# Both state products of a chunk pair at one step in a state-space scan

## The chip, the cores and the metric

The kernel runs on one core of a Trainium2 chip. Its engines are TensorE (PE, with its weight loads as PEld), VectorE (DVE), ScalarE (ACT), GpSimd (POOL) and SyncE (SP, which issues all DMA transfers of this kernel). Each engine works through its own queue in order and waits on semaphores for what another engine or a transfer has to deliver. The metric is the time of one execution on the device in microseconds: the median of the runs.

## The reference, cut to what matters

Two layers follow each other over 2048 tokens of width 1024, all in float32: a Mamba-2 layer and a sliding-window attention layer. The change is in the Mamba-2 layer's scan. There are 8 groups of 4 heads, and per group the sequence is cut into 16 chunks of 128 tokens:

```
states = einsum('bclgn,bcgrl,bclgrp->bcgrpn', Bc, decay_to_end, x)   # one per chunk
chunk_decay = exp(a_cs[..., -1])
def step(h, inp):
    s, d = inp
    return h * d[..., None, None] + s, h                              # h: state BEFORE the chunk
_, h_in = scan(step, h0, (states, chunk_decay))
y_off = einsum('bclgn,bcgrpn,bcgrl->bclgrp', Cc, h_in, exp(a_cs))
y_diag = einsum('bcgrls,bcsgrp->bclgrp', cb * decay, x)
```

A chunk's output reads the state before it (`h_in`), so the state after the very last chunk is computed by the recurrence but read by nothing.

## The kernel before, in words

The sequence is worked in two halves (`hf` 0 and 1) of 1024 tokens, and each half in 8 head groups (`g`). For a group, `ssm_proj` makes six projections B, C, x0, x1, z0, z1, each over two blocks of 512 tokens. A float32 product is made from a high and a low part of each factor in three matmuls (`mm3`, lines 90 to 92: high by high, high by low, low by high). The weights come by DMA (`wraw`), ACT rounds the high part (`whi`, line 150) and POOL subtracts for the low part (`wlo`, line 152). The results are `ps` in PSUM; ACT and DVE turn them into `sx` (convolution and SiLU, lines 736 to 750) or `zz`.

While the projections of one group run, the scan of the group before it runs beside them: `interleave` takes one of the 14 steps of the generator `ssm_scan` after so much projection work. The eight chunks c of a half are handled in pairs. `stage1(c)` transposes x and B of a chunk into PSUM (`pt`, lines 776 to 778) and makes C by B (line 779); DVE forms `xd` and `xw` (lines 783, 786); ACT and POOL split `xw` into `xh` and `xl` (lines 789, 791), ACT and DVE split B into `bh` and `bl` (lines 793, 795). ACT also makes the decays `dec` from `ab`, a row of cumulated decays that a DMA spreads over all partitions (line 764), and `ce`, which takes the place of `ab` (lines 800 to 808).

`state(c)` then makes the chunk's state product `sps` with `mm3`, of 256 columns, in the PSUM tag "st" of one buffer, multiplies the state before it with the chunk's decay on POOL (`hd`, line 820) and adds the two on DVE (`hn`, line 821; line 816 copies where there is no state yet). `outputs(c)` makes the outputs of a pair in `yt` (lines 833 and 838): it reads `dec` and `xd`, and the state before each chunk with `ce`, so for a pair (c, c+1) it needs hn of c-1 and of c. Only after it are the buffers of `ab` free for the loads of chunks c+4 and c+5. The steps of a group are: stage1(0), stage1(1), then for each pair state(c) with stage1(c+2), state(c+1) with stage1(c+3), and outputs(c).

The order of the instructions on each engine is made when the program is built, by a scheduler that takes them by priority as written and by its own estimates. The scan of the last group has no projections beside it but the first pieces of the output projection (`out_piece`), whose weights `out_load` splits on ACT and DVE (lines 222 and 223).

Of the kernel before, what the change touches and what calls it, by code (L numbers as in the profile page):

```python
# [21 lines left out]
P = 128  # L22
# [38 lines left out]
class Trunk:  # L61
# [691 lines left out]
    def ssm_scan(self, sp, yp, tabs, hf, g, res, yT):  # L753


        nc = self.nc
        dt, acs, cd, w2, atd = (tabs[k] for k in ("dt", "acs", "cd", "w2", "atd"))
        abs_, sts = [], []

        def load(c):  # L760
            if c < 8:
                ab = sp.tile([P, 4, P], F32, tag="ab", name="ab", bufs=4)
                j = c * 8 + g
                nc.sync.dma_start(ab.rearrange("p r l -> p (r l)"), atd[j].partition_broadcast(P))
                abs_.append(ab)

        def stage1(c):
            if c > 7:
                return
            ab = abs_[c]  # L770
            s, o = divmod(c, 4)
            sl = slice(o * P, (o + 1) * P)
            x0, x1, Bt, Ct = (res[n, s] for n in ("x0", "x1", "B", "C"))
            pt = (yp.tile([P, 4, P], F32, tag="y", name="pt", bufs=2) if c % 2
                  else self.tp.tile([P, 4, P], F32, tag="tr", name="pt"))
            nc.tensor.transpose(pt[:, 0, :], x0[:, sl], self.ident)
            nc.tensor.transpose(pt[:, 1, :], x1[:, sl], self.ident)
            nc.tensor.transpose(pt[:, 2, :], Bt[:, sl], self.ident)
            nc.tensor.matmul(pt[:, 3, :], Bt[:, sl], Ct[:, sl], start=True, stop=True)
            xv = pt[:, 0:2, :].rearrange("p a (h d) -> p (a h) d", d=64)  # L780
            xd = sp.tile([P, 4, 64], F32, tag="xd", name="xd", bufs=4)
            hb = dt[:, c, 4 * g:4 * g + 4].unsqueeze(2).to_broadcast([P, 4, 64])
            nc.vector.tensor_tensor(xd, xv, hb, ALU.mult)
            xw = sp.tile([P, 4, 64], F32, tag="xw", name="xw", bufs=1)
            hb = w2[:, c, 4 * g:4 * g + 4].unsqueeze(2).to_broadcast([P, 4, 64])
            nc.vector.tensor_tensor(xw, xv, hb, ALU.mult)
            xf = xw.rearrange("p h d -> p (h d)")
            xh = sp.tile([P, 256], F32R, tag="xh", name="xh")
            nc.scalar.activation(xh, xf, AF.Copy)
            xl = sp.tile([P, 256], F32R, tag="xl", name="xl")  # L790
            nc.gpsimd.tensor_tensor(xl, xf, xh.bitcast(F32), ALU.subtract)
            bh = sp.tile([P, P], F32R, tag="bh", name="bh")
            nc.scalar.activation(bh, pt[:, 2, :], AF.Copy)
            bl = sp.tile([P, P], F32R, tag="bl", name="bl")
            nc.vector.tensor_tensor(bl, pt[:, 2, :], bh.bitcast(F32), ALU.subtract)
            cbm = sp.tile([P, P], F32, tag="cbm", name="cbm", bufs=1)
            nc.vector.tensor_tensor(cbm, pt[:, 3, :], self.triu, ALU.mult)
            dec = sp.tile([P, 4, P], F32, tag="dec", name="dec", bufs=4)
            for r in range(4):
                nc.scalar.activation(dec[:, r, :], ab[:, r, :], AF.Relu, scale=-1.0,  # L800
                                     bias=acs[:, c, 4 * g + r:4 * g + r + 1])
            ce = None
            if not (hf == 0 and c == 0):
                ce = ab
                nc.scalar.activation(ce, ab, AF.Exp)  # L805
                nc.gpsimd.tensor_tensor(ce, ce, Ct[:, sl].unsqueeze(1).to_broadcast([P, 4, P]), ALU.mult)  # L806
            nc.scalar.activation(dec, dec, AF.Exp, scale=-1.0)
            nc.vector.tensor_tensor(dec, dec, cbm.unsqueeze(1).to_broadcast([P, 4, P]), ALU.mult)
            sts.append((xd, (bh, bl, xh, xl), dec, ce))

        def state(c, hprev):
            sps = yp.tile([P, 256], F32, tag="st", name="sps")
            self.mm3(sps, *sts[c][1], True, True)
            hn = self.hsave[g] if (hf == 0 and c == 7) else sp.tile([P, 256], F32, tag="hst", name="hn", bufs=3)
            if hprev is None:
                nc.vector.tensor_copy(hn, sps)
            elif not (hf == 1 and c == 7):
                hb = cd[:, c, 4 * g:4 * g + 4].unsqueeze(2).to_broadcast([P, 4, 64])
                hd = sp.tile([P, 4, 64], F32, tag="hd", name="hd", bufs=1)
                nc.gpsimd.tensor_tensor(hd, hprev.rearrange("p (h d) -> p h d", d=64), hb, ALU.mult)  # L820
                nc.vector.tensor_tensor(hn, hd.rearrange("p h d -> p (h d)"), sps, ALU.add)
            return hn

        def outputs(c0, hps):

            yt = yp.tile([P, 2, 2 * P], F32, tag="y", name="yt", bufs=2)
            for u in range(2):
                xd, _, dec, ce = sts[c0 + u]
                for pr in range(2):
                    yo = yt[:, pr, u * P:(u + 1) * P]  # L830
                    for e in range(2):
                        r = 2 * pr + e
                        nc.tensor.matmul(yo[64 * e:64 * e + 64], xd[:, r, :], dec[:, r, :],  # L833
                                         start=True, stop=ce is None)
                    if ce is not None:
                        for e in range(2):
                            r = 2 * pr + e
                            nc.tensor.matmul(yo[64 * e:64 * e + 64], hps[u][:, 64 * r:64 * r + 64], ce[:, r, :],  # L838
                                             start=False, stop=True)
            s, o = divmod(c0, 4)  # L840
            sl = slice(o * P, (o + 2) * P)
            ysb = sp.tile([P, 2, 2 * P], F32, tag="ysb", name="ysb")
            for pr in range(2):
                yv = ysb[:, pr, :]
                nc.vector.scalar_tensor_tensor(yv, res[f"x{pr}", s][:, sl], self.dch[:, 2 * g + pr:2 * g + pr + 1],  # L845
                                               yt[:, pr, :], ALU.mult, ALU.add)
                nc.gpsimd.tensor_tensor(yv, yv, res[f"z{pr}", s][:, sl], ALU.mult)  # L847
            t0 = (8 * hf + c0) * P
            nc.sync.dma_start(
                yT[2 * g * P:(2 * g + 2) * P, t0:t0 + 2 * P].rearrange("(a p) t -> p a t", p=P), ysb)  # L850

        for c in range(4):
            load(c)
        stage1(0)
        yield
        stage1(1)
        yield
        hprev = self.hsave[g] if hf else None
# [174 lines left out]
```

## Time and profile before

| what | value |
| --- | --- |
| median of 3 runs | 2682.56 us (2681.83 to 2687.38) |
| profiled execution | 2682.86 us, of it the span 2681.2 us |
| PE busy | 2570.6 us, 96% |
| PEld busy | 2142.0 us, 80% |
| DVE busy | 1707.9 us, 64% |
| ACT busy | 1266.6 us, 47% |
| POOL busy | 1051.0 us, 39% |
| mean granted TensorE clock | 0.982 |

The span is the time from the first to the last instruction of the profiled execution; the rest of its time lies around it. Busy time is the time in which an engine has an instruction under way. [...] Matmuls are pipelined: a product of 512 columns has a record of 0.39 us, but the next one starts 0.23 us after it, so starts are compared and not records. The scans of the Mamba-2 layer lie between about 100 and 1495 us.

### The profile page before, as it was taken

Reading aid. Unit: us, or ns where it says so; the run is one execution under the profiler, and the core shown is the slowest. Engines: PE = TensorE matmul, PEld = TensorE weight load, DVE = VectorE, ACT = ScalarE, POOL = GpSimd, SP = SyncE. Lnnn points to the kernel's source line nnn. Section 1 sums busy time; section 2 is a strip of 40 time slices with the busy share of each in tenths; the row PEclk is TensorE's granted clock in tenths of the full one; section 3 lists DMA queues with packets and bytes.
Section 4 is the critical chain, followed back from the end, with each engine's and each line's share of the span. In section 5 each row is a group of like instructions: output and inputs, shape, how many; then the busy total and the mean of one; then the engine's idle time right before and its main releaser. Section 6 shows DMA issues by size and latency. Waiting matters only on the chain.

```text
span 2681.2 us, 39280 instructions
## 1 busy us (share of the span) xinstructions
PE 2570.6 (96%) x14307; PEld 2142.0 (80%) x14307; DVE 1707.9 (64%) x3484; ACT 1266.6 (47%) x3015; POOL 1051.0 (39%) x885
## 2 busy tenths in 40 slices
PE   7999999999999899999999999999999999999998
PEld 6877877778777777877787788888888888888787
DVE  6668665766786566666668644447766776767522
ACT  4555455555554455545556432334554454554321
POOL 2354454545544555555556322223222122221222
PEclk9999999999999999999999999999999999999999
DMA  4322222222313222222224432235111131101343
GB/s 122 94 86 67 77 71 78 68 71 75 112 52 108 68 68 74 75 73 71 66 77 137 141 99 97 95 100 170 52 52 40 52 91 52 56 27 52 111 150 121
DMA packets 266658, 224.49 MB, mean 84 GB/s; under 512 B 31136, under 2 KB 229984, under 8 KB 266464
## 3 DMA queue, kind: packets, MB, share of 16 engines
q1 hardware_dynamic: 266464, 221.98, 27.6%
q8 instruction: 113, 1.85, 0.3%
q14 instruction: 81, 0.66, 0.1%
HBM read 179.72 MB, written 42.21 MB: 83 GB/s over the span
## 4 chain that ended last, share of the span: by engine, by line
PE 71%; DVE 10%; DMA 5%; ACT 5%; issue 4%; POOL 4%; SPq 0%; ACTq 0%; POOLq 0%; DVEq 0%
PE u L251 18%; PE ps L90 13%; PE ps L91 13%; PE ps L92 13%; DMA ab<-atd 4%; DVE sx L746 4%; PE sc L421 2%; POOL wlo L152 2%; PE yt L833 2%; PE yt L838 1%; PE ot L467 1%; ACT dec L800 1%; PE tt L449 1%; PE tq L388 1%; PE ot L471 1%
## 5 line engine op out<-in xcount | busy, mean ns | idle before, releaser
L90 PE MATMUL ps<-hi,whi 128*128 128x512 f32 (+1 forms) x1808 | 732.2, 405 | 1.0 <-ACT hi L139 1.0
L92 PE MATMUL ps<-hi,wlo 128*128 128x512 f32 (+1 forms) x1808 | 710.1, 393 | 2.9 <-POOL wlo L152 2.9
L91 PE MATMUL ps<-lo,whi 128*128 128x512 f32 (+1 forms) x1808 | 709.4, 392 | 0.3 <-DVE lo L140 0.3
L92 PEld LDWEIGHTS ps<-hi,wlo 128*128 128x128 f32 x1808 | 344.2, 190 | 79.8 <-POOL wlo L152 4.3
L90 PEld LDWEIGHTS ps<-hi,whi 128*128 128x128 f32 x1808 | 346.0, 191 | 71.5 <-issue 9.4
L91 PEld LDWEIGHTS ps<-lo,whi 128*128 128x128 f32 x1808 | 346.0, 191 | 60.7 <-DVE lo L140 0.8
L746 DVE SCALAR_TENSOR_TENSOR sx<-raw,cw,sx 128x512 f32<-128x512 f32 x384 | 378.0, 985 | 20.2 <-ACT sx L743 17.5
L152 POOL TENSOR_TENSOR wlo<-wraw,whi 128x1024 fp32r<-128x1024 f32 x114 | 282.5, 2478 | 160.2 <-ACT whi L150 151.4
L800 ACT ACTIVATE dec<-ab,acs 128x128 f32<-128x128 f32 x512 | 168.1, 392 | 170.8 <-DMA ab<-atd 160.5
L251 PE MATMUL u<-oh,yh 128*128 128x512 f32 x768 | 241.7, 395 | 0.0
L251 PE MATMUL u<-ol,yh 128*128 128x512 f32 x768 | 239.1, 392 | 0.2 <-DVE ol L223 0.2
L806 POOL TENSOR_TENSOR ab<-ab,sx 128x512 f32<-128x512 f32 x120 | 166.8, 1390 | 184.5 <-ACT ab L805 181.2
L251 PE MATMUL u<-oh,yl 128*128 128x512 f32 x768 | 237.8, 390 | 0.0
L749 ACT ACTIVATE raw<-sx 128x512 f32<-128x512 f32 x128 | 80.6, 630 | 294.3 <-DVE sx L746 275.6
L376 POOL TENSOR_TENSOR qs<-qf,qs 128x256 fp32r<-128x256 f32 x64 | 48.9, 765 | 416.4 <-ACT qs L375 370.5
L235 POOL TENSOR_TENSOR yl<-yr,yh 128x1024 fp32r<-128x1024 f32 (+1 forms) x64 | 119.2, 1862 | 166.9 <-ACT yh L233 166.9
L90 PE MATMUL ps<-qh,hi 128*128 128x384 f32 x512 | 177.8, 348 | 0.1
L91 PE MATMUL ps<-ql,hi 128*128 128x384 f32 x512 | 172.6, 338 | 1.1 <-POOL ql L332 1.1
L92 PE MATMUL ps<-qh,lo 128*128 128x384 f32 x512 | 172.0, 337 | 0.0
L847 POOL TENSOR_TENSOR ysb<-ysb,zz 128x256 f32<-128x256 f32 x128 | 111.2, 886 | 153.8 <-DVE ysb L845 153.8
L251 PEld LDWEIGHTS u<-oh,yl 128*128 128x128 f32 x768 | 144.3, 188 | 32.3 <-issue 0.8
L251 PEld LDWEIGHTS u<-ol,yh 128*128 128x128 f32 x768 | 144.1, 188 | 31.4 <-DVE ol L223 0.7
(217 smaller groups left out, 4745.0 us busy)
## 6 DMA issues: line engine op xcount, KB each, us to landing
wraw<-in_ssm_w_in SPq DMA_DIRECT2D x98, 512.0 KB, 3.9
ab<-atd SPq DMA_DIRECT2D x128, 256.0 KB, 3.8
xt<-in_x SPq DMA_DIRECT2D x32, 512.0 KB, 4.8
yT<-ysb SPq DMA_DIRECT2D x64, 256.0 KB, 2.4
yr<-yT SPq DMA_DIRECT2D x32, 512.0 KB, 3.9
xt<-x SPq DMA_DIRECT2D x32, 512.0 KB, 3.9
oraw<-in_ssm_w_out SPq DMA_DIRECT2D x16, 512.0 KB, 5.9
x<-xt SPq DMA_DIRECT2D x32, 256.0 KB, 2.1
```

Source lines behind the costliest of these rows:

```text
L90: nc.tensor.matmul(ps, sh, mh, start=first, stop=False)
L91: nc.tensor.matmul(ps, sh, ml, start=False, stop=False)
L92: nc.tensor.matmul(ps, sl, mh, start=False, stop=last)
L152: nc.gpsimd.tensor_tensor(lo, raw, hi.bitcast(F32), ALU.subtract)
L235: nc.gpsimd.tensor_tensor(yl, yr, yh.bitcast(F32), ALU.subtract)
L251: nc.tensor.matmul(st["u"][h], y[:, k, :], w[:, j, 512 * h:512 * h + 512], start=k0 + k == 0 and m == 0, stop=k0 + k == kt - 1 and m == 2)
L421: nc.tensor.matmul(sc[:, e, a:], qT[:, 2 * r2 + e, :], kk[:, v, a:], start=v == 0, stop=v == 1)
L746: nc.vector.scalar_tensor_tensor(sx, raw[:, j:j + BLK], self.cw[:, j, ct:ct + 1], sx, ALU.mult, ALU.add)
L749: nc.scalar.activation(th, sx, AF.Tanh)
L800: nc.scalar.activation(dec[:, r, :], ab[:, r, :], AF.Relu, scale=-1.0, bias=acs[:, c, 4 * g + r:4 * g + r + 1])
L806: nc.gpsimd.tensor_tensor(ce, ce, Ct[:, sl].unsqueeze(1).to_broadcast([P, 4, P]), ALU.mult)
L847: nc.gpsimd.tensor_tensor(yv, yv, res[f"z{pr}", s][:, sl], ALU.mult)
```

## The change

Instead of one state product per step, `states(c)` makes the products of both chunks of a pair at the step of the first one, into one PSUM tile of 2 x 256 columns, which is one bank. The additions of the two states stay at their two steps. The decayed state `hd` of chunk c+1 is issued right behind the addition of chunk c (`decayed`), no longer at the step of chunk c+1. And for the last chunk of the second half (`last`) the transpose of B, the operands `xw`, `xh`, `xl`, `bh`, `bl` and the product are left out, since nothing reads its state. The names of the tiles stay; line numbers below line 778 shift.

```diff
             nc.tensor.transpose(pt[:, 1, :], x1[:, sl], self.ident)
-            nc.tensor.transpose(pt[:, 2, :], Bt[:, sl], self.ident)
+            last = hf == 1 and c == 7
+            if not last:
+                nc.tensor.transpose(pt[:, 2, :], Bt[:, sl], self.ident)
...
-            xw = sp.tile([P, 4, 64], F32, tag="xw", name="xw", bufs=1)
...
-            nc.vector.tensor_tensor(bl, pt[:, 2, :], bh.bitcast(F32), ALU.subtract)
+            bx = None
+            if not last:
+                xw = sp.tile([P, 4, 64], F32, tag="xw", name="xw", bufs=1)
...
+                nc.vector.tensor_tensor(bl, pt[:, 2, :], bh.bitcast(F32), ALU.subtract)
+                bx = bh, bl, xh, xl
...
-        def state(c, hprev):
-            sps = yp.tile([P, 256], F32, tag="st", name="sps")
-            self.mm3(sps, *sts[c][1], True, True)
+        def states(c):
+
+            sps = yp.tile([P, 2, 256], F32, tag="st", name="sps")
+            for u in range(2):
+                if sts[c + u][1]:
+                    self.mm3(sps[:, u, :], *sts[c + u][1], True, True)
+            return sps
+
+        def decayed(c, h):
+            if h is None or c > 7 or (hf == 1 and c == 7):
+                return None
+            hd = sp.tile([P, 4, 64], F32, tag="hd", name="hd", bufs=1)
+            hb = cd[:, c, 4 * g:4 * g + 4].unsqueeze(2).to_broadcast([P, 4, 64])
+            nc.gpsimd.tensor_tensor(hd, h.rearrange("p (h d) -> p h d", d=64), hb, ALU.mult)
+            return hd
+
+        def state(c, add, hd):
+
+            if hf == 1 and c == 7:
+                return None, None
             hn = self.hsave[g] if (hf == 0 and c == 7) else sp.tile([P, 256], F32, tag="hst", name="hn", bufs=3)
-            if hprev is None:
-                nc.vector.tensor_copy(hn, sps)
-            elif not (hf == 1 and c == 7):
-                hb = cd[:, c, 4 * g:4 * g + 4].unsqueeze(2).to_broadcast([P, 4, 64])
-                hd = sp.tile([P, 4, 64], F32, tag="hd", name="hd", bufs=1)
-                nc.gpsimd.tensor_tensor(hd, hprev.rearrange("p (h d) -> p h d", d=64), hb, ALU.mult)
-                nc.vector.tensor_tensor(hn, hd.rearrange("p h d -> p (h d)"), sps, ALU.add)
-            return hn
+            if hd is None:
+                nc.vector.tensor_copy(hn, add)
+            else:
+                nc.vector.tensor_tensor(hn, hd.rearrange("p h d -> p (h d)"), add, ALU.add)
+            return hn, decayed(c + 1, hn)
...
         hprev = self.hsave[g] if hf else None
+        hd = decayed(0, hprev)
         for c in range(0, 8, 2):
+            sps = states(c)
             h0 = hprev
-            h1 = state(c, h0)
+            h1, hd = state(c, sps[:, 0, :], hd)
             stage1(c + 2)
             yield
-            hprev = state(c + 1, h1)
+            hprev, hd = state(c + 1, sps[:, 1, :], hd)
             stage1(c + 3)
             yield
             outputs(c, (h0, h1))
```

The names in the order below carry the build's numbers, which differ between the two programs. On PE, in the third group of the first half, the step of chunk 4 before (`sps_3092` is its product, `pt_3100` the transposes of chunk 6):

```order
L90 MATMUL sps_3092<-xh_2914,bh_2918 128x256
L91 MATMUL sps_3092<-xl_2916,bh_2918 128x256
L92 MATMUL sps_3092<-xh_2914,bl_2920 128x256
L776 MATMUL pt_3100<-ident_83,sx_2186 128x128
L777 MATMUL pt_3100<-ident_83,sx_2363 128x128
L778 MATMUL pt_3100<-ident_83,sx_1865 128x128
L779 MATMUL pt_3100<-sx_2036,sx_1865 128x128
L90 MATMUL ps_3085<-hi_262,whi_3018 128x512
L91 MATMUL ps_3085<-lo_263,whi_3018 128x512
L92 MATMUL ps_3085<-hi_262,wlo_3020 128x512
```

and now (`sps_3084` takes both products, first of chunk 4, then of chunk 5):

```order
L90 MATMUL sps_3084<-xh_2910,bh_2914 128x256
L91 MATMUL sps_3084<-xl_2912,bh_2914 128x256
L92 MATMUL sps_3084<-xh_2910,bl_2916 128x256
L90 MATMUL sps_3084<-xh_2972,bh_2976 128x256
L91 MATMUL sps_3084<-xl_2974,bh_2976 128x256
L92 MATMUL sps_3084<-xh_2972,bl_2978 128x256
L776 MATMUL pt_3095<-ident_83,sx_2182 128x128
L777 MATMUL pt_3095<-ident_83,sx_2358 128x128
L780 MATMUL pt_3095<-ident_83,sx_1861 128x128
L781 MATMUL pt_3095<-sx_2033,sx_1861 128x128
```

The three matmuls of chunk 5 have moved up by 18 projection matmuls and stand ahead of the transposes of chunk 6; they stood ahead of those of chunk 7.

On POOL, in the same group, around the operands of chunks 0 and 1 before (`xl_2605` is chunk 0's, `xl_2661` chunk 1's, `wlo_2870` a weight split):

```order
L791 TENSOR_TENSOR xl_2605<-xw_2601,xh_2603 128x256
L152 TENSOR_TENSOR wlo_2870<-wraw_2866,whi_2868 128x1024
L791 TENSOR_TENSOR xl_2661<-xw_2657,xh_2659 128x256
L820 TENSOR_TENSOR hd_2783<-hn_2718,cd_892 128x256
L791 TENSOR_TENSOR xl_2731<-xw_2727,xh_2729 128x256
L820 TENSOR_TENSOR hd_2902<-hn_2782,cd_892 128x256
L791 TENSOR_TENSOR xl_2797<-xw_2793,xh_2795 128x256
```

and now (`xl_2597`, `xl_2653`, `wlo_2863`):

```order
L795 TENSOR_TENSOR xl_2597<-xw_2593,xh_2595 128x256
L152 TENSOR_TENSOR wlo_2863<-wraw_2859,whi_2861 128x1024
L795 TENSOR_TENSOR xl_2653<-xw_2649,xh_2651 128x256
L829 TENSOR_TENSOR hd_2715<-hn_2713,cd_892 128x256
L795 TENSOR_TENSOR xl_2728<-xw_2724,xh_2726 128x256
L829 TENSOR_TENSOR hd_2777<-hn_2775,cd_892 128x256
L795 TENSOR_TENSOR xl_2790<-xw_2786,xh_2788 128x256
```

The weight split still stands between the two, while chunk 1's product, which reads the second, now stands at the step of chunk 0; `hd` of chunk 1 reads the new `hn` of chunk 0 at the same place as before.

On DVE, in the same group, around the additions of chunks 4 (`hn_3096`) and 5 (`hn_3150`) before:

```order
L741 COPY halo_345<-raw_3074 128x3
L746 SCALAR_TENSOR_TENSOR sx_3078<-raw_3074,cw_332,sx_3078 128x512
L750 SCALAR_TENSOR_TENSOR sx_3009<-raw_3005,sx_3009 128x512
L746 SCALAR_TENSOR_TENSOR sx_3078<-raw_3074,cw_332,sx_3078 128x512
L821 TENSOR_TENSOR hn_3096<-hd_3097,sps_3092 128x256
L746 SCALAR_TENSOR_TENSOR sx_3078<-raw_3074,cw_332,sx_3078 128x512
L783 TENSOR_TENSOR xd_3105<-pt_3100,dt_883 128x256
L786 TENSOR_TENSOR xw_3107<-pt_3100,w2_894 128x256
L738 COPY raw_3182<-halo_345 128x3
L750 SCALAR_TENSOR_TENSOR sx_3078<-raw_3074,sx_3078 128x512
L795 TENSOR_TENSOR bl_3115<-pt_3100,bh_3113 128x128
L797 TENSOR_TENSOR cbm_3117<-pt_3100,triu_90 128x128
```

and now (`hn_3091`, `hn_3141`):

```order
L741 COPY halo_345<-raw_3066 128x3
L746 SCALAR_TENSOR_TENSOR sx_3070<-raw_3066,cw_332,sx_3070 128x512
L750 SCALAR_TENSOR_TENSOR sx_3001<-raw_2997,sx_3001 128x512
L746 SCALAR_TENSOR_TENSOR sx_3070<-raw_3066,cw_332,sx_3070 128x512
L840 TENSOR_TENSOR hn_3091<-hd_2961,sps_3084 128x256
L746 SCALAR_TENSOR_TENSOR sx_3070<-raw_3066,cw_332,sx_3070 128x512
L785 TENSOR_TENSOR xd_3100<-pt_3095,dt_883 128x256
L790 TENSOR_TENSOR xw_3102<-pt_3095,w2_894 128x256
L840 TENSOR_TENSOR hn_3141<-hd_3093,sps_3084 128x256
L750 SCALAR_TENSOR_TENSOR sx_3070<-raw_3066,sx_3070 128x512
L799 TENSOR_TENSOR bl_3110<-pt_3095,bh_3108 128x128
L802 TENSOR_TENSOR cbm_3112<-pt_3095,triu_90 128x128
```

Chunk 4's addition keeps its place; chunk 5's has moved up ahead of chunk 6's `bl` and one step of the convolution.

## Rows read from the trace of the kernel before

**Rows 1.** The page's engine table: busy us (share of the span), instructions.
```profile
PE 2570.6 (96%) x14307; PEld 2142.0 (80%) x14307; DVE 1707.9 (64%) x3484; ACT 1266.6 (47%) x3015; POOL 1051.0 (39%) x885
```

**Rows 2.** Busy time by stage: stretch, length, PE PEld DVE ACT POOL (instructions), clock, DMA.
```profile
210.00:735.00 525.00, 500.20 (x2847) 414.29 (x2846) 357.87 (x655) 277.03 (x596) 269.44 (x221) 0.97 0.27 78
...
1495.00:1820.00 325.00, 324.76 (x1436) 266.80 (x1435) 151.22 (x247) 103.76 (x158) 94.14 (x74) 1.00 0.33 108
```

**Rows 3.** Waits of PE: who waited for whom, us in total, times, longest.
```profile
PE sps L90 <- DVE hn L821: 74.1, 19, 7.2
...
PE ps L92 <- POOL wlo L152: 2.9, 2, 1.9
```

**Rows 4.** Timeline of PE, third group: start, us, instruction, [idle before it and releaser].
```profile
331.68 0.28 PE L90 MATMUL sps<-xh,bh 128*128 128x256 f32 x1
...
340.78 0.55 PE L90 MATMUL sps<-xh,bh 128*128 128x256 f32 x1 [3.91 <-DVE hn L821]
...
348.65 0.44 PE L833 MATMUL yt<-dec,xd 128*64 128x128 f32 x4
...
354.76 0.28 PE L90 MATMUL sps<-xh,bh 128*128 128x256 f32 x1
```

**Rows 5.** Timeline of all engines, 329 to 341 us.
```profile
329.94 1.01 SPq L764 DMA_DIRECT2D ab<-atd  x2
...
334.47 1.57 ACT L800 ACTIVATE dec<-ab,acs 128x128 f32<-128x128 f32 x5 [3.19 <-DMA ab<-atd]
...
336.60 0.17 DVE L741 COPY halo<-raw 128x3 f32<-128x3 f32 x1 [2.40 <-ACT raw L739]
...
340.22 0.41 DVE L821 TENSOR_TENSOR hn<-hd,sps 128x256 f32<-128x256 f32 x1
```

**Rows 6.** Busy time and clock in windows from a late state product on.
```profile
147.36:154.90 7.54, 7.54 (x26) 6.17 (x26) 7.45 (x14) 3.12 (x7) 4.59 (x5) 0.66 0.00 0
...
340.78:348.60 7.82, 7.82 (x32) 6.55 (x32) 7.82 (x14) 3.96 (x9) 7.04 (x6) 0.81 0.09 23
...
1337.05:1345.10 8.05, 8.05 (x32) 6.69 (x32) 8.05 (x12) 5.54 (x12) 7.84 (x7) 0.79 0.01 2
```

**Rows 7.** Timeline of PE after a shorter wait, end of the first half.
```profile
812.60 0.35 PE L90 MATMUL sps<-xh,bh 128*128 128x256 f32 x1 [2.67 <-DVE hn L821]
```

**Rows 8.** Timeline of PE, chunk 0's product and transposes, third group; later group's product.
```profile
298.21 0.28 PE L90 MATMUL sps<-xh,bh 128*128 128x256 f32 x1
298.33 0.28 PE L91 MATMUL sps<-xl,bh 128*128 128x256 f32 x1
...
298.57 0.27 PE L776 MATMUL pt<-ident,sx 128*128 128x128 f32 x1
298.68 0.27 PE L777 MATMUL pt<-ident,sx 128*128 128x128 f32 x1
...
1292.01 0.28 PE L90 MATMUL sps<-xh,bh 128*128 128x256 f32 x1
```

**Rows 9.** Timeline of POOL, chunk 1's operand in the third group and a later one.
```profile
296.63 2.39 POOL L152 TENSOR_TENSOR wlo<-wraw,whi 128x1024 fp32r<-128x1024 f32 x1 [4.85 <-ACT whi L150]
298.98 1.26 POOL L791 TENSOR_TENSOR xl<-xw,xh 128x256 fp32r<-128x256 f32 x1
...
1292.77 1.20 POOL L791 TENSOR_TENSOR xl<-xw,xh 128x256 fp32r<-128x256 f32 x1
```

**Rows 10.** Timeline of POOL, third group, around chunk 7's operand.
```profile
346.52 1.06 POOL L820 TENSOR_TENSOR hd<-hn,cd 128x256 f32<-128x256 f32 x1
348.37 0.73 POOL L791 TENSOR_TENSOR xl<-xw,xh 128x256 fp32r<-128x256 f32 x1 [0.78 <-ACT xh L789]
```

**Rows 11.** Timeline of PE and DVE, last group of the first half, chunks 6 and 7.
```profile
803.92 0.28 PE L90 MATMUL sps<-xh,bh 128*128 128x256 f32 x1
...
806.43 0.28 DVE L795 TENSOR_TENSOR bl<-pt,bh 128x128 fp32r<-128x128 f32 x1
```

**Rows 12.** Waits of PE in the last scan, 1441 to 1495 us.
```profile
PE sps L90 <- DVE hn L821: 4.9, 2, 3.5
```

**Rows 13.** Timeline of DVE in the last scan.
```profile
1463.29 3.48 DVE L223 SCALAR_TENSOR_TENSOR ol<-oraw,gn,oh 128x1024 fp32r<-128x1024 f32 x2
```

More of the change, by code (lines that the diff above doesn't have):

```diff
@@ L783, in stage1 @@
             nc.vector.tensor_tensor(xd, xv, hb, ALU.mult)
-            xw = sp.tile([P, 4, 64], F32, tag="xw", name="xw", bufs=1)
[L785 to L794, printed above, removed]
-            nc.vector.tensor_tensor(bl, pt[:, 2, :], bh.bitcast(F32), ALU.subtract)
+            bx = None
+            if not last:
+                xw = sp.tile([P, 4, 64], F32, tag="xw", name="xw", bufs=1)
+                hb = w2[:, c, 4 * g:4 * g + 4].unsqueeze(2).to_broadcast([P, 4, 64])
+                nc.vector.tensor_tensor(xw, xv, hb, ALU.mult)
+                xf = xw.rearrange("p h d -> p (h d)")
+                xh = sp.tile([P, 256], F32R, tag="xh", name="xh")
+                nc.scalar.activation(xh, xf, AF.Copy)
+                xl = sp.tile([P, 256], F32R, tag="xl", name="xl")
+                nc.gpsimd.tensor_tensor(xl, xf, xh.bitcast(F32), ALU.subtract)
+                bh = sp.tile([P, P], F32R, tag="bh", name="bh")
+                nc.scalar.activation(bh, pt[:, 2, :], AF.Copy)
+                bl = sp.tile([P, P], F32R, tag="bl", name="bl")
+                nc.vector.tensor_tensor(bl, pt[:, 2, :], bh.bitcast(F32), ALU.subtract)
+                bx = bh, bl, xh, xl
             cbm = sp.tile([P, P], F32, tag="cbm", name="cbm", bufs=1)
@@ L808, in stage1 @@
             nc.vector.tensor_tensor(dec, dec, cbm.unsqueeze(1).to_broadcast([P, 4, P]), ALU.mult)
-            sts.append((xd, (bh, bl, xh, xl), dec, ce))
-        def state(c, hprev):
-            sps = yp.tile([P, 256], F32, tag="st", name="sps")
-            self.mm3(sps, *sts[c][1], True, True)
-            hn = self.hsave[g] if (hf == 0 and c == 7) else sp.tile([P, 256], F32, tag="hst", name="hn", bufs=3)
-            if hprev is None:
-                nc.vector.tensor_copy(hn, sps)
-            elif not (hf == 1 and c == 7):
-                hb = cd[:, c, 4 * g:4 * g + 4].unsqueeze(2).to_broadcast([P, 4, 64])
-                hd = sp.tile([P, 4, 64], F32, tag="hd", name="hd", bufs=1)
-                nc.gpsimd.tensor_tensor(hd, hprev.rearrange("p (h d) -> p h d", d=64), hb, ALU.mult)
-                nc.vector.tensor_tensor(hn, hd.rearrange("p h d -> p (h d)"), sps, ALU.add)
-            return hn
+            sts.append((xd, bx, dec, ce))
+        def states(c):
[14 more added lines that the diff above has]
+                return None, None
+            hn = self.hsave[g] if (hf == 0 and c == 7) else sp.tile([P, 256], F32, tag="hst", name="hn", bufs=3)
+            if hd is None:
[3 more added lines that the diff above has]
+            return hn, decayed(c + 1, hn)
         def outputs(c0, hps):
```

## The prediction, made before the changed kernel ran

> **What bounds the kernel now.** I read the engine table of the page first, then the busy time by stage, then TensorE's own waits, then the timeline around the largest wait. TensorE is busy 96% of the span [rows 1], so little can be won but its idle time. By stage the idle time is uneven: the stretch of the six scans in the middle of the first half (210 to 735) has 24.8 us without a matmul and a granted clock of 0.97, the output stage (1495 to 1820) has 0.2 us and 1.00 [rows 2]. TensorE's list of waits says where this sits: 74.1 us, in 19 waits, the longest 7.2 us, are the first matmul of a state product (sps, L90) waiting for the state addition on DVE (hn, L821) [rows 3]. All of TensorE's idle time is 2681.2 less 2570.6, 110.6 us, so this one wait is two thirds of it.
>
> Its cause shows in the third head group, whose chunk 4 makes its product at 331.68. Chunk 5's product starts only at 340.78, 3.91 us after TensorE is free [rows 4]. The product needs the one PSUM buffer of the tag "st", and that is held until DVE has added chunk 4's state, at 340.22 to 340.63 [rows 5]. DVE is late because its queue stands: the load of chunk 6's ab starts at 329.94 behind SP's queue, ACT's decay for it waits 3.19 us for that load until 334.47, the copy of the projection stands behind it on ACT, DVE's halo copy waits 2.40 us for that until 336.60, and hn stands behind the halo on DVE [rows 5]. Nothing of this is TensorE's work; only the single buffer ties it to TensorE.
>
> **Part 1, the wait that goes.** In the new order both products of a pair stand together and the 18 projection matmuls follow without a state product between them. TensorE then needs hn of chunk 4 first in the outputs of chunks 4 and 5, at 348.65 before [rows 4]. Take the 3.91 us off, the slow clock below (1.5 us) and the 0.36 us of the product that has moved: TensorE arrives at about 342.9 and hn is there at 340.6, 2.3 us early. DVE's and ACT's rows there do not wait for TensorE, so hn keeps its time, and DVE's order has it on the same place. In general TensorE has 6.0 us of work ahead of that need (348.65 less 340.78, less 1.5 and 0.36), and of the 19 waits only the longest, 7.2 us, is longer: 1.2 us of it stays. I take 74.1 less the tail's 4.9 [rows 3, 12], 69.2 us, as gone.
>
> **Part 2, the clock.** After the long waits TensorE restarts at the lower of its two levels. The window from the restart at 340.78 to the outputs has a granted clock of 0.81 over 7.82 us: 7.82 x 0.19 is 1.5 us lost. I took the same window behind each of the 13 waits of 3.47 us or more outside the tail; three are shown (0.66, 0.81, 0.79) [rows 6], and length times missing clock sums to 30.7 us. The waits of 1.2 to 2.7 us lose nothing: after 2.67 us the product takes 0.35 us, not 0.55 [rows 7, 4]. So 30.7 us go with the waits.
>
> **Part 3, dropped work.** In each of the 8 groups of the second half the last chunk loses three state matmuls and a transpose. On TensorE these advance by 0.12 us and 0.11 us each [rows 8], so 8 x (3 x 0.12 + 0.11) = 3.8 us. What ACT, DVE and POOL save beside it is off the path.
>
> **Part 4, waits that are added.** The first pair is now multiplied at the place where only chunk 0 was, so chunk 1's operands are due one step, about 5 us, earlier. In the third group TensorE would reach chunk 1's second matmul at 298.21 + 4 x 0.12 = 298.69 [rows 8]. That matmul reads xl, which POOL delivers at 298.98 + 1.26 = 300.24, because the weight split wlo (2.39 us) stands ahead of it [rows 9], and in the new POOL order it still does. The wait is 1.55 us. Queued behind it on TensorE are the transposes of chunk 2 and all projections: it is paid in full. The same subtraction in every group gives 1.47 to 1.55 us at eleven places (the last: xl at 1292.77 + 1.20 = 1293.97, TensorE at 1292.01 + 0.48 = 1292.49 [rows 8, 9]), 1.0 and 0.3 at the two groups that open a half, none at the others: 18.0 us. For the later pairs the operands were made two steps ahead. In the first half TensorE would want chunk 7's xl at about 354.76 - 3.91 - 1.5 - 0.36 + 0.48 = 349.5, and it ends at 349.10 [rows 4, 10]; the early hd on POOL stands ahead of chunk 6's xl and may cost up to 1 us here, in six groups. I take 0 and keep 0 to 6 us. At the end of the first half chunk 7's bl ends at 806.71 and TensorE wants it at 803.92 + 5 x 0.12 = 804.52: 2.2 us more [rows 11]. In the second half chunk 7 has no product.
>
> [...]
>
> **Part 5, the decayed state.** hd is the same operation on POOL (1.06 us [rows 10]), as often as before, now issued right behind the hn that it reads. For POOL that is a wait on DVE, and behind it stand xl, the gating product ce and wlo. In the order it mostly moves past one xl. I cost it at nothing, because what reads hd (the next hn) is not on TensorE's path now. In the second half the order also puts wlo ahead of chunk 5's xl; that frees the raw weights earlier and so lets SP issue the ab load earlier, which can only shorten the DVE delay above.
>
> **Part 6, the tail.** In the last scan, which runs between output pieces, TensorE waits 4.9 us for hn [rows 12]. There the addition stands behind two weight products of 3.48 us on DVE [rows 13] and still does; only 6 matmuls lie between the new product and the outputs that need it. That wait moves to the outputs. With one wait of 1.45 us gone and a later bl for chunk 1 added, I take 0, bounds -5 and +6 us.
>
> **The sum.** Gone: 69.2 + 30.7 + 3.8 = 103.7. Added: 18.0 + 2.2 + 1.2 = 21.4. Net 82.3 us. The profiled execution took 2682.86 us, of which 2681.2 is the span and 1.66 lies around it and stays: 2682.86 - 82.3 = 2600.6, forecast 2601 us. The median of the runs is 2682.56, 0.3 us beside the profiled one, which I neglect.
>
> **Rivals.**
> First, the wait moves on. DVE's late stretch stays, and with TensorE some 5 us faster per group DVE has less time to catch up; it is busy 68% of the stage now [rows 2] and would be 72%. If DVE ran 3 us later against TensorE, the outputs or the last pair's products would wait in each of 12 groups: some 36 us back, 2637 us. For it speaks that slacks are 2.3 us and less; against it that the projections of z behind chunk 7 need little of DVE.
>
> Second, the new waits do not come, because POOL gets xl out ahead of wlo: 18 us more gained, 2583 us. The order speaks against it.
>
> Third, the half clock after the short waits too: 13 x 2.4 us (30.7 over 13) is 31 us, 2632 us. Rows 7 speak against it.
>
> Fourth, slower. POOL stands at hd until TensorE has made the product and DVE has added it, and everything behind it slips: six weight splits a group come late and TensorE's projections themselves wait for wlo. Today that wait is 2.9 us in 2 cases [rows 3]. It decides from 82.3 us over 14 groups x 6 splits, about 1.0 us each; at 1.2 us each it is 101 us and the time 2701. Against it: in the order a split stands behind the moved hd only once or twice in a group, and its weights are used a sixth of a group (525 us for 6 groups [rows 2], so 14.6 us) after the split before them.
>
> Fifth, the change does not do what it says: the pair's single bank still makes TensorE wait for hn, only at the next pair, and just the dropped work counts: 2679 us. The distance speaks against it: hn of chunk 4 is there at 340.6, that of chunk 5 can follow it at once, and the next pair's product would come at 349 [rows 4, 5].
>
> **How the numbers follow.** Forecast 0.60, its own range 2590 to 2612 (tail -5 to +6, chunk 7 up to 6, new waits 2 either way). First rival 0.20, second 0.06, third 0.08, fourth 0.04, fifth 0.02. Runs tell a change from none at about 0.2%, 5 us: faster 0.94, same 0.02 (the fifth), slower 0.04 (the fourth). The range 2586 to 2638 takes in the forecast, the first and the third and leaves out the other three, 0.12, and some of the edges.
>
> **What would show it.** In the profile after: sps waiting for hn gone or under 8 us in TensorE's list; a new entry of 15 to 20 us in which the state product waits for POOL's xl, in about 13 waits of 1.5 us; the granted clock at 0.99 or more in the scans; the period of a group in the first half down from 87.5 us (525 over 6) to about 83; 120 state products instead of 128. I am wrong if the outputs (L833, L838 before) or the products take up a wait for hn or for xl of chunk 7, if ps waits for wlo grow past 10 us, or if the clock stays at 0.97.

## The result and the profile after

The changed kernel takes 2639.89 us (median of 4 runs, 2635.28 to 2643.13) against 2682.19 us for the kernel before on the same chip: ratio 0.9837, 95% interval 0.9816 to 0.9858. That is 42 us faster, where 82 were forecast; the time lies 1.9 us above the upper end of the range. The profiled execution took 2643.13 us with a span of 2641.2, 40.0 less than before.

The engine table of the page after (busy us, share, instructions) answers to [rows 1]:

```profile
PE 2559.0 (97%) x14275; PEld 2128.8 (81%) x14275; DVE 1699.3 (64%) x3468; ACT 1262.2 (48%) x2999; POOL 1027.3 (39%) x877
```

TensorE's busy time fell by 11.6 us and its idle time (span less busy) by 28.4, from 110.6 to 82.2. TensorE's waits after (who waited for whom, us in total, times, longest) answer to [rows 3]:

```profile
PE sps L91 <- POOL xl L795: 30.3, 18, 2.5
PE sps L90 <- ACT bh L797: 17.1, 10, 3.5
...
PE ps L92 <- POOL wlo L152: 1.6, 2, 1.3
...
PE sps L92 <- DVE bl L799: 0.9, 1, 0.9
...
PE yt L857 <- DVE hn L840: 0.3, 1, 0.3
```

The wait for hn is gone, in the outputs too. In its place the state product waits 48.3 us for its operands. Most of it, 35.5 us, stands at one place, chunk 1's product in the first pair of a group (11.4 us in the first half, 24.1 in the second, the last scan left out). Another 6.0 us stand at chunk 5's product in the group that opens each half, and 6.3 in the last scan. PE's timeline shows the first place, first in the third group of the first half and then in the third group of the second:

```profile
290.84 0.28 PE L90 MATMUL sps<-xh,bh 128*128 128x256 f32 x1
...
292.90 0.39 PE L91 MATMUL sps<-xl,bh 128*128 128x256 f32 x1 [1.43 <-POOL xl L795]
...
992.13 0.38 PE L90 MATMUL sps<-xh,bh 128*128 128x256 f32 x1 [2.15 <-ACT bh L797]
...
994.96 0.58 PE L91 MATMUL sps<-xl,bh 128*128 128x256 f32 x1 [2.44 <-POOL xl L795]
```

The first is the wait of the forecast (1.55 us there), the other two are 4.6 us and were not expected. Windows of 8 us from such waits on (the column ahead of the last two is the granted clock, a share of full speed) answer to [rows 6, 7]:

```profile
292.90:300.90 8.00, 8.00 (x41) 6.79 (x42) 7.86 (x18) 2.87 (x7) 2.42 (x3) 1.00 0.23 65
...
543.10:551.10 8.00, 8.00 (x34) 6.87 (x35) 6.31 (x16) 2.48 (x5) 2.41 (x3) 0.79 0.21 63
994.96:1002.96 8.00, 8.00 (x29) 6.71 (x30) 5.32 (x14) 2.48 (x5) 2.41 (x3) 0.66 0.23 66
```

The records of both kernels have the clock at 1.00 or at 0.50 and nowhere between: in the kernel before, behind the 3.91 us of [rows 4], at 0.50 from 341.0 to 343.0 us and at 1.00 from 344.0 to 348.6; in the third window here at 0.50 to 1000.4 us and at 1.00 from 1001.0. A value between them is a mean over the window. The third start lies behind 2.15 and 2.44 us of waiting, the second behind 2.53, the first behind 1.43. In the same way the ten waits of 1.77 us and more with a slow window behind them cost 22.0 us of clock. One of the ten is in the last scan. The prediction's 13 waits of before, 30.7 us, leave the last scan out; with its wait of 3.50 us, which has this window behind it, they are 33.8:

```profile
1467.25:1475.25 8.00, 8.00 (x47) 6.84 (x48) 6.62 (x13) 3.21 (x10) 4.73 (x5) 0.61 0.75 233
```

The sum of the prediction, term by term:

| term | forecast, us | measured, us |
| --- | --- | --- |
| waits of the state product, gone less added | 69.2 - 21.4 = 47.8 | 76.0 - 48.3 = 27.7 |
| half clock | 30.7 | 33.8 - 22.0 = 11.8 |
| dropped work | 3.8 | 3.8 taken (5.1 in a run of its own) |
| sum | 82.3 | 43.3, spans 40.0 |

(76.0 is 74.1 for hn and 1.9 for dec.) The measured terms are 3.3 us more than the spans show; where these stayed is not known. By halves, the start of the second half's first group comes 27.3 us earlier than before, and all that follows adds 12.7 to it. The period of a group tells where the rest stayed. It is the mean over five groups, second to seventh, from one chunk 0 product to the next, in all kernels of this study:

| kernel | us | first half | second half |
| --- | --- | --- | --- |
| before | 2682.2 | 87.3 | 88.7 |
| after | 2639.9 | 84.0 | 87.1 |
| drop_only | 2680.9 | 87.4 | 88.4 |
| all_apart | 2679.8 | 87.5 | 88.7 |
| first_apart | 2620.4 | 81.8 | 84.4 |
| after_ab6 | 2610.4 | 82.7 | 82.3 |
| before_ab6 | 2622.6 | 83.1 | 81.2 |
| apart_ab6 | 2592.2 | 81.0 | 80.7 |
| ab_pool_queue | 2659.8 | 84.0 | 87.6 |
| apart_ab_pool_queue | 2639.9 | 83.3 | 85.1 |
| after_wr3 | 2653.9 | 83.9 | 87.4 |
| apart_wr3 | 2635.6 | 82.0 | 85.6 |
| raw_pool_queue | 2629.1 | 82.7 | 86.5 |
| apart_raw_pool_queue | 2589.5 | 81.0 | 81.0 |

In the second half TensorE lost its largest wait and the group became only 1.6 us shorter. Why is seen in all engines' timeline from the outputs of chunks 4 and 5 to the first pair of the next group (SPq is SyncE, which starts the transfers):

```profile
955.31 2.86 POOL L152 TENSOR_TENSOR wlo<-wraw,whi 128x1024 fp32r<-128x1024 f32 x1
...
955.38 0.39 PE L857 MATMUL yt<-ab,hn 128*64 128x128 f32 x4
...
958.20 0.38 SPq L148 DMA_DIRECT2D wraw<-in_ssm_w_in  x1
...
958.62 1.05 SPq L764 DMA_DIRECT2D ab<-atd  x2
...
969.23 1.04 ACT L150 ACTIVATE whi<-wraw 128x1024 fp32r<-128x1024 f32 x1
...
970.35 2.40 POOL L152 TENSOR_TENSOR wlo<-wraw,whi 128x1024 fp32r<-128x1024 f32 x1 [0.68 <-ACT whi L150]
...
972.78 0.38 SPq L148 DMA_DIRECT2D wraw<-in_ssm_w_in  x1
973.26 1.00 SPq L764 DMA_DIRECT2D ab<-atd  x2
...
978.09 1.57 ACT L805 ACTIVATE dec<-ab,acs 128x128 f32<-128x128 f32 x5 [7.33 <-DMA ab<-atd]
...
984.10 0.58 ACT L739 ACTIVATE raw<-ps 128x512 f32<-128x512 f32 x1
...
984.72 0.71 DVE L741 COPY halo<-raw 128x3 f32<-128x3 f32 x1 [1.86 <-ACT raw L739]
...
991.05 0.42 DVE L790 TENSOR_TENSOR xw<-pt,w 128x256 f32<-128x256 f32 x1
...
991.43 2.35 POOL L152 TENSOR_TENSOR wlo<-wraw,whi 128x1024 fp32r<-128x1024 f32 x1 [4.09 <-ACT whi L150]
...
993.74 1.17 POOL L795 TENSOR_TENSOR xl<-xw,xh 128x256 fp32r<-128x256 f32 x1
```

The outputs free their ab buffers at about 955.8, but the loads into them, for chunks 0 and 1 of the next group, start at 958.62: SP first has to start a raw weight load, and that waits for wlo until 958.17. Two steps on it repeats for chunks 2 and 3 (wlo to 972.75, wraw 972.78, ab 973.26). ACT waits 7.33 us for that load; its copies and decays, and DVE behind them, come late, so whi and wlo come late, so the next raw weight load, so the next ab. These engines turn in a loop beside TensorE. In the kernel before, the loads for chunks 2 and 3 start while the outputs still run, and the same two ends of the chain stand further from TensorE's need:

```profile
1005.63 1.21 SPq L764 DMA_DIRECT2D ab<-atd  x2
...
1006.08 0.39 PE L838 MATMUL yt<-ab,hn 128*64 128x128 f32 x4
...
1009.60 1.28 ACT L800 ACTIVATE dec<-ab,acs 128x128 f32<-128x128 f32 x4 [5.76 <-DMA ab<-atd]
...
1025.41 0.28 PE L90 MATMUL sps<-xh,bh 128*128 128x256 f32 x1
...
1026.17 1.19 POOL L791 TENSOR_TENSOR xl<-xw,xh 128x256 fp32r<-128x256 f32 x1
```

From chunk 2's decay, behind which chunk 0's and 1's operands stand in ACT's queue, to TensorE's first product there are 15.8 us before and 11.4 after (978.09 to 989.47). TensorE gained 4.4 us on the loop, and pays them at the next place where it needs something from it.

### The profile page after: what moved, and what is told of

The parts are those of the page before. It is cut to its first block, busy times and chain, and to the rows that moved or that the text cites. A ratio compares the mean times of both kernels' runs of the same rounds, so it can differ in the third digit from the quotient of the medians.

```text
span 2641.2 us, 39193 instructions
## 1 busy us (share of the span) xinstructions
PE 2559.0 (97%) x14275; PEld 2128.8 (81%) x14275; DVE 1699.3 (64%) x3468; ACT 1262.2 (48%) x2999; POOL 1027.3 (39%) x877
## 4 chain that ended last, share of the span: by engine, by line
PE 63%; DVE 12%; POOL 7%; ACT 6%; DMA 6%; issue 5%; SPq 1%; ACTq 0%; POOLq 0%; DVEq 0%
PE u L251 18%; PE ps L90 11%; PE ps L91 11%; PE ps L92 11%; DMA ab<-atd 4%; DVE sx L746 4%; POOL wlo L152 3%; PE sc L421 2%; DVE dec L813 2%; ACT dec L805 1%; POOL ab L811 1%; ACT whi L150 1%; PE ot L467 1%; PE tt L449 1%; PE yt L852 1%
## 5 line engine op out<-in xcount | busy, mean ns | idle before, releaser
L746 DVE SCALAR_TENSOR_TENSOR sx<-raw,cw,sx 128x512 f32<-128x512 f32 x384 | 360.5, 939 | 22.3 <-ACT sx L743 18.9
L749 ACT ACTIVATE raw<-sx 128x512 f32<-128x512 f32 x128 | 80.7, 630 | 287.8 <-DVE sx L746 283.4
L233 ACT ACTIVATE yh<-yr 128x1024 fp32r<-128x1024 f32 (+1 forms) x64 | 54.1, 845 | 240.0 <-PE u L251 178.0
```

Of the source, the lines that this page charges most:

```text
L233: nc.scalar.activation(yh, yr, AF.Copy)
L746: nc.vector.scalar_tensor_tensor(sx, raw[:, j:j + BLK], self.cw[:, j, ct:ct + 1], sx, ALU.mult, ALU.add)
L749: nc.scalar.activation(th, sx, AF.Tanh)
```

## The experiments

Theory A says that only the early place of chunk 1's product is wrong; theory B that the loop bounds the group. Each ratio is to the kernel before, run on the same chip.

**first_apart**

```diff
-        def states(c):
+        def states(c, n):
...
-            for u in range(2):
+            for u in range(n):
...
-            sps = states(c)
+            sps = states(c, 1 if c == 0 else 2)
...
             yield
+            if c == 0:
+                self.mm3(sps[:, 1, :], *sts[1][1], True, True)
             hprev, hd = state(c + 1, sps[:, 1, :], hd)
```

> The changed kernel with one edit: in the first pair of each group the product of chunk 1 stands at its own step again, in the other half of the same bank; the later pairs stay together. Theory A (the place): TensorE is held only because chunk 1's operands (bh of ACT, xl of POOL) are wanted one step too early. Then nearly all of the 48.3 us of waits for xl and bh go, and with them most of the 25 us that the half clock costs now: about 2585 us, and a group of the second half takes some 83 us. Theory B (the loop): in the second half the work of SP, ACT and POOL (raw weight load, behind it the load of ab, the decays, whi, wlo, and the next raw weight load) needs about 88.6 us for a group by itself, wherever TensorE waits for it. Then only the waits of the first half go (14.8 us and about 5 us of clock): about 2620 us, a group of the second half stays at 88 us, and TensorE waits at another place of it.

Measured: 2620.36 us, ratio 0.9757 (0.9737 to 0.9776). That is B's total but not its split: both halves gained, 2.2 us a group in the first and 2.7 in the second. TensorE's waits and one row of its timeline:

```profile
PE sps L91 <- POOL xl L795: 10.7, 11, 2.5
PE sps L90 <- DVE hn L840: 8.7, 5, 2.5
```

```profile
983.57 0.36 PE L90 MATMUL sps<-xh,bh 128*128 128x256 f32 x1 [2.50 <-DVE hn L840]
```

As B has it, a wait comes back elsewhere: chunk 1's product now waits for hn in five groups of the second half. A falls. But the loop is not fixed at 88.6 us either, so B as it was put falls too; TensorE's outputs, which free the buffers of ab, are probably a part of it (raw_pool_queue below bears on this).

**after_ab6 and before_ab6**

```diff
-        self.px = self.pool(ctx, "px", 4)
+        self.px = self.pool(ctx, "px", 3)
...
-                ab = sp.tile([P, 4, P], F32, tag="ab", name="ab", bufs=4)
+                ab = sp.tile([P, 4, P], F32, tag="ab", name="ab", bufs=6)
...
-        for c in range(4):
+        for c in range(6):
             load(c)
...
-            load(c + 4)
-            load(c + 5)
+            load(c + 6)
+            load(c + 7)
```

> The changed kernel with six buffers for ab in place of four, so that the loads of ab are issued one pair earlier and no longer stand behind a raw weight load when they are wanted; to make room the pool of x tiles has three buffers, not four. Theory A (the place): the order at the first pair is the same, TensorE still reaches chunk 1's product 2 to 5 us before its operands: 2640 us, within 8. Theory B (the loop): ACT no longer waits for ab, the loop gets shorter than TensorE's own work, the 15 us of waits for bh go and those for xl fall back to the 1.5 us that chunk 1's place costs (about 20 us in all): 2600 to 2610 us, a group of the second half at 84 to 86 us.

Measured: 2610.37 us, ratio 0.9717 (0.9701 to 0.9732). ACT's waits for ab, in the kernel before, in the changed one and here:

```profile
ACT dec L800 <- DMA ab<-atd: 160.5, 66, 7.1
```

```profile
ACT dec L805 <- DMA ab<-atd: 169.1, 67, 7.6
```

```profile
ACT dec L805 <- DMA ab<-atd: 4.3, 1, 4.3
```

TensorE's waits here and two rows of its timeline:

```profile
PE sps L91 <- POOL xl L795: 24.2, 20, 2.5
PE sps L90 <- ACT bh L797: 2.5, 4, 1.0
```

```profile
296.92 0.39 PE L91 MATMUL sps<-xl,bh 128*128 128x256 f32 x1 [1.43 <-POOL xl L795]
...
981.45 0.38 PE L91 MATMUL sps<-xl,bh 128*128 128x256 f32 x1 [1.36 <-POOL xl L795]
```

With the loads early, eleven groups show the forecast's wait, 1.43 us in the first half and 1.36 in the second, where the prediction had worked out 1.47 to 1.55. The clock is 1.00 behind it. This shows what is left of B: the lateness beyond it came from ab.

The x tile given up costs some 10 us of this time. From the last state product to the end of the span there are 1199.1 us, after 1195.3, and the first state product starts 6.7 us later (the changed kernel, then this one):

```profile
118.64 0.28 PE L90 MATMUL sps<-xh,bh 128*128 128x256 f32 x1
```

```profile
125.38 0.28 PE L90 MATMUL sps<-xh,bh 128*128 128x256 f32 x1
```

All five kernels with three x tiles start it at 125.1 to 125.9 us, and those with four at 118.2 to 119.2 (121.2 with the raw loads on POOL), whatever else they change.

> The kernel before, its state products and decayed state unchanged, with the same six buffers of ab and earlier loads (and three x tiles). If the late load of ab is what makes hn late (the cause that the prediction gives for the 74.1 us of waits), these waits fall under 20 us and half clock after them goes: 2682 less about 55 less about 25, near 2600 us. If DVE is late for another reason (its own work, POOL's port, the projections), the waits stay above 50 us and the time is 2670 to 2685 us.

Measured: 2622.59 us, ratio 0.9767 (0.9751 to 0.9783). TensorE's wait for hn, 74.1 us before:

```profile
PE sps L90 <- DVE hn L821: 26.1, 14, 2.5
```

It falls by 48 us but not under 20: 1.8 us stay in each middle group of the first half, and none in the second to sixth group of the second. ACT waits 3.9 us for ab in all here, so the late ab made about two thirds of the wait for hn, as the prediction had it; what makes the rest is open. Of the other reasons that the expectation names, a port of POOL's is shown by no run: in the trace of before the same operation on DVE (dec, L808) took 2.83 us at 431.01, where wlo ran on POOL, and 0.68 us at 436.30, where POOL was idle, and why is not seen there. Without touching a state product the early loads bring more than the change did: 0.9767 against 0.9837.

**drop_only**

```diff
+            last = hf == 1 and c == 7
+            if not last:
+                nc.tensor.transpose(pt[:, 2, :], Bt[:, sl], self.ident)
...
+            if hf == 1 and c == 7:
+                return None
```

> The kernel before with only the last part of the change: the unread state of the last chunk and what feeds it is dropped. By the prediction's term this is worth 3.8 us of TensorE's work alone: 2678 us. If what is dropped on DVE, ACT and POOL counts too, because these run behind TensorE in the second half: 2665 to 2673 us.

Measured: 2680.86 us, ratio 0.9981 (0.9971 to 0.999), 2.7 to 7.8 us. The term of 3.8 lies in it; a further gain from DVE, ACT or POOL, to 9 us and more in all, is out.

**all_apart**

```diff
-        def states(c):
+        def states(c, n):
...
-            for u in range(2):
+            for u in range(n):
...
-            sps = states(c)
+            sps = states(c, 1)
...
             yield
+            if sts[c + 1][1]:
+                self.mm3(sps[:, 1, :], *sts[c + 1][1], True, True)
```

> The changed kernel with every product at its own step, as in the kernel before; of the change there stay the PSUM tile with two halves of one bank, the early decayed state and the dropped last state. If it is the second half (a place to write while DVE has not yet read the first) that took the wait for hn away, and not the early place of the product, the waits of sps for hn stay under 15 us, those for xl and bh are small too, and the time is that of first_apart, 2620 us, within 10. If the place matters (with the product at its own step the bank is still held until hn is added), the waits for hn are 60 us and more again: 2665 to 2680 us.

Measured: 2679.77 us, ratio 0.9983 (0.9974 to 0.9993). TensorE's first wait:

```profile
PE sps L90 <- DVE hn L840: 73.4, 18, 6.2
```

A second place to write is worth nothing while it lies in the same tile: the product into the other half waits for hn as before (73.4 us against 74.1). The gain of the change comes from both products standing ahead of DVE's first read. That the tile is one bank, and whether the wait stands there for the bank or only for the tile, no run here shows. This kernel also keeps the early decayed state, and its ratio is that of drop_only (0.9983 against 0.9981): the early decayed state brings nothing here that stands out of the noise.

**ab_pool_queue and apart_ab_pool_queue** (the first on the changed kernel, the second on first_apart)

```diff
-                nc.sync.dma_start(ab.rearrange("p r l -> p (r l)"), atd[j].partition_broadcast(P))
+                nc.gpsimd.dma_start(ab.rearrange("p r l -> p (r l)"), atd[j].partition_broadcast(P))
```

> The changed kernel, four buffers of ab, but its loads are issued by POOL and not by SP, so that none stands behind a raw weight load. If it is the place behind the raw weight load in SP's queue that makes ab late (about 3 us a load, by the trace of the changed kernel), waits for bh go and xl falls to about 1.5 us a group, as with six buffers: 2605 to 2620 us. If it is the buffer that comes free late (outputs on TensorE), the time stays within 8 us of 2640; if issuing costs POOL more than 1 us each, wlo and xl get later and it is slower than 2640.

> Chunk 1's product at its own step, and the loads of ab issued by POOL with four buffers and four x tiles. If the queue is what makes ab late, this does what apart_ab6 does and keeps the x tiles, worth some 4 us after the scans: about 2584 us. If POOL pays for the issues, 2600 us or more.

Measured: 2659.82 us, ratio 0.9909 (0.9894 to 0.9924), and 2639.93 us, 0.9834 (0.982 to 0.9849): each 20 us slower than with SP's queue. The timeline of the first shows why nothing is gained (the outputs of chunks 4 and 5, then the load for the next group):

```profile
969.22 2.84 POOL L152 TENSOR_TENSOR wlo<-wraw,whi 128x1024 fp32r<-128x1024 f32 x1
969.39 0.39 PE L857 MATMUL yt<-ab,hn 128*64 128x128 f32 x4
...
972.00 1.12 POOL L764 DMA_DIRECT2D ab<-atd  x2
```

On POOL the load stands right behind the same wlo that held it on SP. The test did not separate what it was meant to; it shows that POOL's queue was no way around this wait for POOL. The 20 us themselves are not explained by this. On the changed kernel the middle groups keep their period to 0.5 us; of the 17.6 us between the spans, 3.8 are lost in the first group of all, 6.3 between the seventh and the eighth group of the first half and 4.5 in the last scan. The cause there is open; the issues take POOL 0.59 us each in the median.

**after_wr3 and apart_wr3** (again on the changed kernel and on first_apart; the tag "wr" has three buffers wherever it is used, and there are three x tiles)

```diff
-        raw = self.wp.tile([P, kt, cols], F32, tag="wr", name="wraw")
+        raw = self.wp.tile([P, kt, cols], F32, tag="wr", name="wraw", bufs=3)
...
-        self.px = self.pool(ctx, "px", 4)
+        self.px = self.pool(ctx, "px", 3)
```

> The changed kernel with three buffers for the raw weights in place of two (and three x tiles), SP's order of weights and ab unchanged, ab with its four buffers. A raw weight load then no longer waits at SP for the last split's wlo. If that wait, with the ab load behind it, is the link that closes the loop, ab is issued as soon as the outputs free its buffer, some 3 us earlier each time; waits for bh go, those for xl fall to 1.4 us a group: 2610 to 2618 us, a group of the second half at 83 to 85 us. If the buffer that the outputs free is what makes ab late, the time stays at 2640 to 2646 us (the x tiles cost some 4 us after the scans).

> The same third raw weight buffer, and chunk 1's product at its own step. If the wait of the raw weights closes the loop: as apart_ab6, 2590 to 2600 us, with no wait of sps above 2 us in the middle groups. If not: 2620 us as first_apart, with waits for hn or xl of 2 us in the second half.

Measured: 2653.86 us, ratio 0.9886 (0.9868 to 0.9903), and 2635.58 us, 0.9815 (0.9788 to 0.9842): some 14 and 15 us slower than with two buffers. Most of that is the price of the x tile given up, some 10 us as above. From the first to the last state product after_wr3 takes 1327.7 us and the changed kernel 1327.3, so the third raw buffer does nothing there; with chunk 1 apart it costs 6.5 us (1310.9 against 1304.4). The expectation was wrong about the buffer. All engines' timeline of the first:

```profile
1033.86 2.38 POOL L152 TENSOR_TENSOR wlo<-wraw,whi 128x1024 fp32r<-128x1024 f32 x1 [2.24 <-ACT whi L150]
...
1036.26 0.37 SPq L148 DMA_DIRECT2D wraw<-in_ssm_w_in  x1
1036.73 1.00 SPq L764 DMA_DIRECT2D ab<-atd  x2
```

SP still starts the raw load when wlo ends (1036.24). With a third buffer the loads seem to run one weight further ahead and to wait for the same wlo, at the same place in the queue.

**raw_pool_queue and apart_raw_pool_queue**

```diff
-        nc.sync.dma_start(raw, src.rearrange("(k p) c -> p k c", p=P))
+        nc.gpsimd.dma_start(raw, src.rearrange("(k p) c -> p k c", p=P))
         hi = self.wp.tile([P, kt, cols], F32R, tag="wh", name="whi")
```

> The changed kernel with four buffers of ab as it has, loaded by SP; the raw weights are loaded by POOL, behind the split that frees their buffer, so that nothing stands ahead of ab on SP but stores of the pair before. If ab is late because of the raw weight load in front of it (by the trace of the changed kernel about 3 us a load, four times a group), the waits for bh go and xl falls to about 1.5 us in the middle groups: 2608 to 2625 us, less what 98 issues cost POOL (the ab issues took 0.57 us each, off TensorE's path unless xl stands behind one). If ab is late because the outputs free its buffer late, the waits of the changed kernel stay: 2640 us or more, and only the earlier load with six buffers can help.

> The same, with chunk 1's product at its own step. If the raw weight load in front is the cause: 2590 to 2605 us, without the cost of three x tiles after the scans. If the late free buffer is the cause: 2620 us as first_apart, or more.

Measured: 2629.09 us, ratio 0.9791 (0.9768 to 0.9814), and 2589.51 us, 0.9648 (0.9631 to 0.9664). All engines' timeline of the first, and TensorE's waits of the second:

```profile
1049.47 0.39 PE L857 MATMUL yt<-ab,hn 128*64 128x128 f32 x4
1049.50 1.20 SPq L764 DMA_DIRECT2D ab<-atd  x2
...
1053.36 0.99 ACT L805 ACTIVATE dec<-ab,acs 128x128 f32<-128x128 f32 x3 [5.69 <-DMA ab<-atd]
```

```profile
PE sps L90 <- ACT bh L797: 4.5, 2, 3.5
PE sps L91 <- POOL xl L795: 3.9, 4, 2.5
```

Now ab starts while the outputs still run. In the middle groups of the first half that is all that was wrong: each wait is 1.43 us, the period 82.7, as in after_ab6. In those of the second half about 0.9 us for bh and 2.4 for xl stay as long as chunk 1 stands early; there the buffer that comes free only with the outputs counts too, since the earlier loads of after_ab6 take these waits away. With chunk 1 at its own step this slack is enough, and both halves run at 81.0 us. The weight loads take POOL 0.93 us each in the median, where the expectation reckoned with 0.57.

**apart_ab6** (the edits of first_apart and after_ab6 together)

> Both edits: chunk 1's product at its own step, and six buffers of ab with loads a pair earlier (three x tiles). Theory B (the loop): with ab early the only waits left are the 1.4 us at chunk 1's early place in each middle group, 24 us in all for xl, and this edit removes them without a new wait: 2610 - 22 = 2588 us, a group of either half at 81 to 82 us. If the loop is still the limit, the wait comes back at another place (hn or ps for wlo) and the time is 2600 to 2612 us.

Measured: 2592.24 us, ratio 0.9662 (0.9645 to 0.9678): no new wait in any middle group. It and apart_raw_pool_queue beat both kernels; their intervals overlap. From the first to the last state product it is the shorter of the two (1265.8 us against 1274.1), and it pays for the x tile outside.

## Why the prediction was right or wrong

**Right: what goes.** hn of chunk 4 is early enough for the outputs: they wait 0.3 us in all. The wait fell by 74.1 us, 5 more than the term, since the tail's part went too; there waits of 6.3 us for operands came instead, so that the tail gives nothing, as forecast, though not by a wait at the outputs. The ab load as the cause of the late hn is shown by before_ab6 for 48 of the 74 us, the dropped work by drop_only. The 2.2 us for chunk 7 at the end of the first half came as 0.5 us.

**Wrong: the size of the new waits**, in the step "The same subtraction in every group gives 1.47 to 1.55 us at eleven places". It set the times of POOL's xl in the trace of before against an earlier need on TensorE, as if only TensorE's time could change. But in that trace TensorE was held back 3.5 to 7 us a group by the very loop that makes xl; with the wait gone TensorE comes earlier and the loop hardly does (in the second half 1.6 us a group). The waits came to 48.3 us instead of 21.4; with what went, 20.1 us of the forecast are missing here. That about 1.4 of the 1.5 us is right once ab is early is shown by after_ab6. The sentence "DVE's and ACT's rows there do not wait for TensorE, so hn keeps its time" held the answer: what keeps its time while TensorE moves up is late one step on. The first rival had this mechanism and 2637 us, with 0.20, but looked for it at the outputs and the last pair; it stands at the next group's first pair, behind the decays of its own ab loads. That its number lies so near is luck: it puts all of its 36 us down to waits, where nearly half of what is missing is clock. Of the prediction's signs of being wrong only the clock came near (0.98 in the scans, 100 to 1455 us, where 0.99 was forecast and 0.97 would have spoken against it). Its sign of being right, an entry of 15 to 20 us for xl, came as 30.3 us with 17.1 for bh beside it.

**Wrong: the clock.** Of 33.8 us, the last scan's 3.1 among them, 11.8 came back. "The waits of 1.2 to 2.7 us lose nothing" rested on one row, a wait of 2.67 us [rows 7]; the new waits of 2.44 to 2.53 us, five times with a wait of 0.45 to 2.15 us one matmul ahead, end in windows at 0.63 to 0.80, those of 1.4 and 2.0 us, and one of 2.38, at 1.00. This is the third rival at the longer waits only. So some short waits have a fall of the clock behind them and others, of 1.4 to 2.4 us, have none; what decides between them, no run here shows.

**The rest.** The second rival is out, since the new waits came. The waits at chunk 7's xl stayed away and POOL's hd delayed no weight split that TensorE waited for (ps waits 1.6 us for wlo), so the fourth rival is out. What the early hd does beside the joined products was not run; with the products apart it does nothing that stands out of the noise (all_apart). The fifth is out: the wait for hn is gone. Open is which of the chain's steps between ab and bh makes the 0.9 us that raw_pool_queue keeps in the second half.

## What to carry to other kernels

When a wait is taken from the busiest engine, the other engines' times in the old trace cannot simply be kept (here waits of 48.3 us came where 21.4 were worked out from them): ask first which loop of queues, buffers and loads made them late, and whether it runs on without that engine. Look at what stands ahead of a load in its issuing queue; here a weight load that waited for a split held the small load behind it (to 958.62 us, with its buffer free at about 955.8), and loading that earlier was, alone, worth more than the reordering of the products (0.9767 against 0.9837). Two halves of one PSUM tile were one buffer here as far as waiting goes (73.4 us for hn in all_apart). And look at the price of an edit that only makes room: the x tile given up for more buffers cost some 10 us outside the stretch that was studied.

## What the runs showed of the hardware

The clock behind a wait does not follow from that wait's length alone: after one wait of 2.67 us the window was at 1.00 [rows 7], after one of 2.53 at 0.79, after 2.00 and 0.52 close together at 1.00, after 1.16 and 1.77 at 0.79. A load of ab started by POOL took 0.59 us of POOL in the median (ab_pool_queue), one started by SP 0.42 us of SP (the changed kernel), and its median time to landing was 5.0 us against 4.5; for the weight loads it was 4.8 us (raw_pool_queue) against 4.0.
